# One down product behind the first plain tile, and the last norm's sums by VectorE and ScalarE

## Chip, core and metric

The kernel runs on one core of a Trainium2 chip. The metric is the device time of one execution in microseconds (us), as the median of several runs. TensorE (PE in the rows, PEld for its weight loads), VectorE (DVE), ScalarE (ACT), GpSimd (POOL) and the DMA queue of SyncE (SP) each work through their own instructions in order and wait for each other by semaphores.

## What is computed

One layer on 1024 tokens of width 1024, in float32 with products split into a high and a low part. What the change touches is the first and the third of its three residual steps and the norm behind the last:

```python
def layer_norm(x, g, b):
    mu = jnp.mean(xf, axis=-1, keepdims=True)
    var = jnp.mean(jnp.square(xf - mu), axis=-1, keepdims=True)
    y = (xf - mu) * lax.rsqrt(var + LN_EPS)
    return (y * g + b).astype(x.dtype)

def swiglu_ffn(x, w_gate, w_up, w_down):
    return (jax.nn.silu(x @ w_gate) * (x @ w_up)) @ w_down

x = layer_norm(ALPHA * x + 0.5 * swiglu_ffn(x, ...1), ln1_g, ln1_b)
x = layer_norm(ALPHA * x + hybrid_mixer(x, ...), ln2_g, ln2_b)
x = layer_norm(ALPHA * x + 0.5 * swiglu_ffn(x, ...2), ln3_g, ln3_b)
```

## The kernel before

Activations lie with features on the 128 partitions and tokens along the row, in halves of 512 tokens; each FFN (`Ffn`, once with `idx` 0 and once with `idx` 2) holds eight accumulators `acc[d][h]` per half. The order of TensorE's instructions is the order in which the code issues them (`run` walks a generator); the other engines' orders come from a scheduler that works with priorities, and `hoist()` raises one.

The down projection has two parts. `down` (L742) makes 2x2 block products with seven instead of eight multiplications over twelve of the 22 hidden tiles: for each item `(j0, m)` a PSUM tile `X` takes one product after the other, and after each of them `gather` (L693) adds `X` to an accumulator on VectorE (L696). The next product is added onto the same `X`, so TensorE may not start it before that addition has read `X`. In the loop another product always stands between two products onto the same tile. The last pass of the loop (`it` is None) has no item of its own any more: it issues the product with `s3` (9 matmuls, 3 tiles by 3 split terms), `gather`, then the product with `a22` (9 matmuls) and `gather`. With `idx` 2 a postponed product (`late_s1`) stands between these two; with `idx` 0 nothing does.

Behind `down`, `go` runs the plain tiles of the remaining hidden tiles (`plain`, L671): for each `d` 18 matmuls into a new PSUM tile of pool `dense` (4 slots), 6 hidden tiles by 3 split terms, with weights that `last_weights` splits on ScalarE and VectorE (L131, L132; the last two of a tile's six weight pieces lie in a shared tile `rest`), and hidden tiles that SP has fetched from DRAM (L794).

The last norm is done with tokens on the partitions. `TokenNorm.part(i)` transposes four accumulators to two PSUM tiles of 128 x 512, one for each 128 tokens (L363), and makes the sums `s` and the sums of squares `q`. In general `s` comes from a reduction on VectorE (L367) and `q` from a Square with an accumulated sum on ScalarE (L371). Only in the second part of the last 256 tokens (`own`) does TensorE make `s`: 8 products of an accumulator with a column of ones (L357), ahead of the transposes. `stats` (L386) then works on 128 x 2 numbers; `apply` (L399) makes four results from the four PSUM tiles (L402) and scales them (L411), and SP writes each to DRAM.

Of the kernel before, what the change touches and what calls it, by code (L numbers as in the profile page):

```python
# [8 lines left out]
F32 = mybir.dt.float32  # L9
# [3 lines left out]
AF = mybir.ActivationFunctionType  # L13
# [5 lines left out]
P = 128  # L19
# [48 lines left out]
def hybrid_layer(ctx, tc, xT, wg1, wu1, wds1, wd1, wg2, wu2, wds2, wd2, wcol, wnv, wgv, wdl, wgate,  # L68
                 wbr, wout, lnp, bias, dec2, bdec, ng, ident_d, masks_d, ln3, outN):
    nc = tc.nc  # L70
# [4 lines left out]
    def pool(stack, name, bufs=1, space=None):  # L75
        kw = dict(name=name, bufs=bufs)
        if space is not None:
            kw["space"] = space
        if space is not DRAM:
            kw["reuse_waits"] = "tile"  # L80
        return stack.enter_context(tc.tile_pool(**kw))
# [5 lines left out]
    lp = pool(ctx, "lp")  # L87
# [7 lines left out]
    def nm(s):  # L95
        uid[0] += 1
        return f"{s}_{uid[0]}"
# [29 lines left out]
    def dps(shape=(P, HF)):  # L127
        return dense.tile(list(shape), F32, tag="d", name=nm("d"))
# [46 lines left out]
    ones = cpool.tile([P, P], F32, tag="ones", name="ones")  # L175
# [13 lines left out]
    def run(*streams):  # L189
        for st_ in streams:  # L190
            for cost in st_:
                clock[0] += cost
                while pending and pending[0][0] <= clock[0]:
                    pending.pop(0)[2]()
# [134 lines left out]
    class TokenNorm:  # L329
# [20 lines left out]
        def part(self, i):  # L350
            s, q = ((self.s0, self.q0), (self.s1, self.q1))[i]
            own = i and self.t0 == S - TOK
            if own:
                self.s1 = s = dps((P, 2))
                for t in range(2):
                    for d in range(4):
                        nc.tensor.matmul(s[:, t:t + 1], self.z[4 + d][:, t * P:(t + 1) * P],  # L357
                                         ones[:, 0:1], start=d == 0, stop=d == 3)
            ps = [aux.tile([P, HF], F32, tag=t, name=nm("tz"), bufs=b)
                  for t, b in ((("pt", 1), ("o", 1)), (("s", 2), ("s", 2)))[i]]  # L360
            for d in range(4):
                for t in range(2):
                    nc.tensor.transpose(ps[t][:, d * P:(d + 1) * P],  # L363
                                        self.z[4 * i + d][:, t * P:(t + 1) * P], ident)
            for t in range(2):
                if not own:
                    nc.vector.tensor_reduce(s[:, t:t + 1], ps[t], axis=AX.X, op=ALU.add)  # L367
                if i == 0:
                    nc.vector.tensor_scalar(self.nc[:, t:t + 1], s[:, t:t + 1], -1.0 / HF, None,
                                            ALU.mult)  # L370
                nc.scalar.activation(self.tmp_(), ps[t], AF.Square, bias=self.nc[:, t:t + 1],  # L371
                                     accum_out=q[:, t:t + 1])
            if i == 0:
                self.ps = [ps]
                nc.vector.tensor_scalar(self.e, q, 0.25 / D, self.eps / 4, ALU.mult, ALU.add)
            else:
                self.ps.append(ps)
# [46 lines left out]
    def tagged(pl, tags, bufs):  # L424
        c = [0]

        def alloc(dt=F32):
            c[0] += 1
            t = tags[c[0] % len(tags)]
            return pl.tile([P, HF], dt, tag=t, name=nm(t), bufs=bufs)  # L430
        return alloc
# [7 lines left out]
    class Ffn:  # L439
# [287 lines left out]
        def down(self):  # L727
            prev, B, nxt = None, None, self.operands(0)
            self.wait = []
            items = [(j0, m) for j0 in range(0, PAIRS, NP) for m in range(4)]  # L730
            for it in [*items, None]:
                if it:
                    j0, m = it
                    if m == 0:
                        B, nxt = nxt, None
                    w = self.down_factors(j0, m)
                    if m == 1:
                        if j0 + NP < PAIRS:
                            nxt = self.operands(j0 + NP)
                        else:  # L740
                            for f in LAST:
                                self.fetch(f, 0)  # L742
                    X = dps()
                    yield from self.product(X, w["a11"], B[0], True)
                    self.gather(2 * m, 0, X)
                    Y = dps()
                    yield from self.product(Y, w["a12"], B[1], True)
                    self.gather(2 * m, 0, Y)
                if prev:
                    pm, pX, pw, pB = prev  # L750
                    yield from self.product(pX, pw["s3"], pB[5])
                    self.gather(2 * pm + 1, 1, pX)
                    if not it and self.idx:
                        yield from self.late_s1(self.wait[-1])
                late = it and j0 + NP == PAIRS and m > 1
                if late:
                    self.wait.append([m, w, B])
                elif it:
                    Z = dps()
                    yield from self.product(Z, w["s1"], B[3], True)  # L760
                    self.gather(2 * m + 1, 1, Z)
                if it:
                    yield from self.product(X, w["s2"], B[4])
                    self.gather(2 * m, 1, X)
                if prev:
                    yield from self.product(pX, pw["a22"], pB[6])
                    self.gather(2 * pm + 1, 0, pX)
                if it:
                    if not late:
                        yield from self.product(Z, w["s4"], B[2])  # L770
                        self.gather(2 * m, 1, Z)
                    prev = m, X, w, B
# [23 lines left out]
        def go(self, first, parts, sink_of):  # L796
            head = 2
            w2 = []
            for f in (0, 1):
                ws = first if f == 0 and first else self.gate_up(f)  # L800
                run(self.glu(f, ws, 0))
                w2.append(ws)
            for f in (0, 1):
                run(self.glu(f, w2[f], 1))
            for i in range(4):
                self.sums_of(i)
            run(self.blocks(range(head, FT)))
            self.front()
            run(self.down())
            idx, acc, tmp = self.idx, self.acc, self.tmp  # L810
            sums = tagged(self.hp, ("sr",), 4)
            dead = lambda dt=F32: xpool.tile([P, HF], dt, tag="x", name=nm("dead"))
            for f in LAST:
                self.fetch(f, 1)
            wr = self.last_weights()
            if idx:
                gb = [dead() for _ in range(4)]
                for i, t in enumerate(gb):
                    nc.sync.dma_start(t, ln3[0:1, i * HF:(i + 1) * HF].to_broadcast([P, HF]))
                token = lambda t0: TokenNorm(4 * LN_EPS, tmp, dead, gb, t0)  # L820
            for n, (h, c0, cn) in enumerate(parts):
                ln = None
                if idx == 0:
                    lags, gap = ln_lags[idx, h]
                    ln = Norm(cn, idx, 4 * LN_EPS, sums, tmp, sink_of(h, c0, cn), lags, gap)
                elif n == len(parts) - 1:
                    ln = token(h * HF + c0)
                for d in range(KD):
                    run(self.plain(LAST, d, next(wr) if n == 0 else self.wr[d], h, c0, cn))
                    if ln:  # L830
                        ln.add(acc[d][h][:, c0:c0 + cn])
                if not ln:
                    for i, c in enumerate(range(c0, c0 + cn, TOK)):
                        token(h * HF + c).later([acc[d][h][:, c:c + TOK] for d in range(KD)],
                                                TN_T0 + TN_DT * i)
                if n == 0:
                    run(self.deferred())
# [711 lines left out]
```

## Time and profile before

| | |
|---|---|
| Median of 3 runs | 2069.66 us (2068.62 to 2070.48) |
| The profiled execution | 2069.46 us, its span 2067.7 us |
| Granted TensorE clock, mean | 0.998 |
| PE busy, share of the span | 99% |
| PEld | 81% |
| DVE | 67% |
| ACT | 43% |
| POOL | 8% |
| DMA, mean | 155 GB/s |

The trace's times count from the span's start. In a timeline row the first two numbers are the start and the duration in us, then come engine, line, operation, tile written <- tiles read, the shape and, as xN, how many equal instructions the row merges; what stands in square brackets is the idle time of that engine just before, and what ended it.

### The profile page before, as it was taken

How to read it: one execution, taken by the hardware profiler on the slowest of the kernel's cores; microseconds unless marked ns; L12 is line 12 of the kernel's file. 1: busy time of each engine (PE TensorE's matmuls, PEld its weight loads, DVE VectorE, ACT ScalarE, POOL GpSimd, SP SyncE). 2: the span in 40 equal slices, each digit the busy share in tenths (PEclk: the TensorE clock that was granted, in tenths of full speed). 3: DMA queues.
4: the chain of work that ended last, by engine and by line, in shares of the span. 5: the costliest groups of instructions: out<-in, count | busy, mean ns of one | idle time of the engine just before them, and what ended most of it. 6: DMA issues, size and time to landing. Idle time of an engine off the chain costs nothing.

```text
span 2067.7 us, 26798 instructions
## 1 busy us (share of the span) xinstructions
PE 2046.2 (99%) x9738; PEld 1684.6 (81%) x9738; DVE 1378.0 (67%) x2355; ACT 896.1 (43%) x1502; POOL 159.1 (8%) x243
## 2 busy tenths in 40 slices
PE   9999999999999999999999999999999999999998
PEld 7888888888888788877788888887888888888888
DVE  8676776547668875236557755799767777457647
ACT  6444444322224554346656544355544444322212
POOL 0000000000013221213100000132000000000000
PEclk9999999999999999999999999999999999999999
DMA  4343444386641354488543336421334443396622
GB/s 145 141 164 131 170 149 134 128 286 248 227 137 49 109 194 138 138 235 228 156 119 107 110 126 194 133 83 73 135 138 153 166 157 126 122 326 220 239 100 83
DMA packets 159765, 321.37 MB, mean 155 GB/s; under 512 B 18448, under 2 KB 42768, under 8 KB 159632
## 3 DMA queue, kind: packets, MB, share of 16 engines
q1 hardware_dynamic: 140304, 274.03, 39.3%
q0 software_dynamic: 9216, 29.37, 4.9%
q10 hardware_dynamic: 10112, 16.26, 2.5%
q8 instruction: 77, 1.26, 0.3%
q14 instruction: 56, 0.46, 0.1%
HBM read 222.19 MB, written 101.06 MB: 156 GB/s over the span
## 4 chain that ended last, share of the span: by engine, by line
PE 83%; issue 6%; DVE 5%; POOL 2%; DMA 2%; ACT 1%; SPq 0%; ACTq 0%; POOLq 0%; DVEq 0%
PE d L569 16%; PE d L567 16%; PE d L568 16%; PE d L122 6%; PE d L124 6%; PE d L123 6%; PE d L674 3%; PE d L676 3%; PE d L675 3%; PE pt L1126 1%; PE po L1143 1%; POOL xl L420 1%; POOL qks L912 1%; DMA gv<-sl 1%; PE d L898 1%
## 5 line engine op out<-in xcount | busy, mean ns | idle before, releaser
L131 ACT ACTIVATE wh<-raw 128x512 fp32r<-128x512 f32 (+4 forms) x148 | 111.5, 763 | 187.6 <-PE d L568 85.4
L132 DVE TENSOR_TENSOR wl<-raw,wh 128x512 fp32r<-128x512 f32 (+4 forms) x148 | 125.3, 854 | 100.4 <-ACT wh L131 100.2
L696 DVE TENSOR_TENSOR a<-a,d 128x512 f32<-128x512 f32 (+1 forms) x152 | 99.9, 657 | 93.8 <-PE d L569 64.7
L123 PE MATMUL d<-xl,wh 128*128 128x512 f32 x384 | 150.7, 392 | 3.6 <-POOL xl L420 3.1
L122 PE MATMUL d<-xh,wh 128*128 128x512 f32 x384 | 153.6, 400 | 0.2
L124 PE MATMUL d<-xh,wl 128*128 128x512 f32 x384 | 150.4, 392 | 0.5 <-DVE wl L112 0.5
L569 PE MATMUL d<-hh,hl 128*128 128x512 f32 x384 | 149.5, 389 | 0.0
L569 PE MATMUL d<-xh,wl 128*128 128x512 f32 x384 | 149.5, 389 | 0.0
L568 PE MATMUL d<-xl,wh 128*128 128x512 f32 x384 | 149.4, 389 | 0.0
L567 PE MATMUL d<-hh,hh 128*128 128x512 f32 x384 | 149.4, 389 | 0.0
L567 PE MATMUL d<-xh,wh 128*128 128x512 f32 x384 | 149.4, 389 | 0.0
L567 PE MATMUL d<-a,wh 128*128 128x512 f32 x384 | 149.4, 389 | 0.0
L568 PE MATMUL d<-a,wh 128*128 128x512 f32 x384 | 149.4, 389 | 0.0
L569 PE MATMUL d<-a,wl 128*128 128x512 f32 x384 | 149.4, 389 | 0.0
L568 PE MATMUL d<-hl,hh 128*128 128x512 f32 x384 | 149.4, 389 | 0.0
L131 ACT ACTIVATE hh<-sr 128x512 fp32r<-128x512 f32 x168 | 105.9, 631 | 83.6 <-DVE sr L508 24.2
L674 PE MATMUL d<-hh,wh 128*128 128x512 f32 (+1 forms) x368 | 134.3, 365 | 0.0
L676 PE MATMUL d<-hh,wl 128*128 128x512 f32 (+1 forms) x368 | 133.0, 361 | 0.0
L675 PE MATMUL d<-hl,wh 128*128 128x512 f32 (+1 forms) x368 | 133.0, 361 | 0.0
L132 DVE TENSOR_TENSOR hl<-sr,hh 128x512 fp32r<-128x512 f32 x168 | 114.9, 698 | 2.2 <-ACT hh L131 1.4
L112 DVE TENSOR_TENSOR wl<-raw,wh 128x512 fp32r<-128x512 f32 (+1 forms) x77 | 81.1, 1054 | 46.6 <-ACT wh L111 42.7
L131 ACT ACTIVATE oh<-hr 128x512 fp32r<-128x512 f32 x88 | 55.4, 631 | 128.4 <-DVE hr L599 44.3
(339 smaller groups left out, 4900.9 us busy)
## 6 DMA issues: line engine op xcount, KB each, us to landing
raw<-in_wu SPq DMA_DIRECT2D x44, 512.0 KB
raw<-in_wg SPq DMA_DIRECT2D x43, 512.0 KB
ops<-oh SPq DMA_DIRECT2D x84, 256.0 KB
ops<-ol SPq DMA_DIRECT2D x84, 256.0 KB
oh<-ops SPq DMA_DIRECT2D x48, 256.0 KB
ol<-ops SPq DMA_DIRECT2D x48, 256.0 KB
hid<-oh SPq DMA_DIRECT2D x40, 256.0 KB
hid<-ol SPq DMA_DIRECT2D x40, 256.0 KB
```

The source lines that it names most:

```text
L122: nc.tensor.matmul(ps, a, xh, start=k == 0, stop=False)
L123: nc.tensor.matmul(ps, a, xl, start=False, stop=False)
L124: nc.tensor.matmul(ps, wl[:, k * m:(k + 1) * m], xh, start=False, stop=k == n - 1)
L131: nc.scalar.activation(hi, src, AF.Copy)
L132: nc.vector.tensor_tensor(lo, src, hi.bitcast(F32), ALU.subtract)
L567: nc.tensor.matmul(ps, a, xh, start=first and k == 0, stop=False, **sg)
L568: nc.tensor.matmul(ps, a, xl, start=False, stop=False, **sg)
L569: nc.tensor.matmul(ps, wl[:, k * P:(k + 1) * P], xh, start=False, stop=k == n - 1, **sg)
L674: nc.tensor.matmul(ps, wh, hi, start=k == 0, stop=False)
L675: nc.tensor.matmul(ps, wh, lo, start=False, stop=False)
L676: nc.tensor.matmul(ps, wl, hi, start=False, stop=k == n - 1)
L696: nc.vector.tensor_tensor(a, a, ps, ALU.add)
```

## The change

Two edits.

First: in the last pass of `down` the `a22` product and its `gather` are no longer issued there when `idx` is 0 but kept as a generator, `self.rest`, and `go` runs it behind the first plain tile of the first block.

Second: for `own`, the 8 products with ones are dropped. `s` becomes an SBUF tile `ln_s1` of pool `lp`; its column 0 comes from a VectorE reduction of the first transposed tile, its column 1 from a ScalarE Copy with an accumulated sum over the second, issued ahead of the two Squares. In the built program `lp` grows by 32 bytes in each partition for it, and the pools opened later (`hp` of both FFNs, and those of the mixer) start 32 bytes further on.

```diff
@@ TokenNorm.part
             if own:
-                self.s1 = s = dps((P, 2))
-                for t in range(2):
-                    for d in range(4):
-                        nc.tensor.matmul(s[:, t:t + 1], self.z[4 + d][:, t * P:(t + 1) * P],
-                                         ones[:, 0:1], start=d == 0, stop=d == 3)
+                self.s1 = s = lp.tile([P, 2], F32, tag="ln_s1", name=nm("ln_s1"), bufs=1)
...
+            if own:
+                nc.scalar.activation(self.tmp_(), ps[1], AF.Copy, accum_out=s[:, 1:2])
             for t in range(2):
-                if not own:
+                if not own or t == 0:
                     nc.vector.tensor_reduce(s[:, t:t + 1], ps[t], axis=AX.X, op=ALU.add)
@@ Ffn.down
                 if prev:
-                    yield from self.product(pX, pw["a22"], pB[6])
-                    self.gather(2 * pm + 1, 0, pX)
+                    def last(pm=pm, pX=pX, pw=pw, pB=pB):
+                        yield from self.product(pX, pw["a22"], pB[6])
+                        self.gather(2 * pm + 1, 0, pX)
+                    if it or self.idx:
+                        yield from last()
+                    else:
+                        self.rest = last()
@@ Ffn.go
                     run(self.plain(LAST, d, next(wr) if n == 0 else self.wr[d], h, c0, cn))
+                    if not (n or d or idx):
+                        run(self.rest)
```

Line numbers of the changed kernel are lower by 2 in most of the code (L696 is L694 there), by 4 for the transposes (L359). In what follows `d_4937` is the tile `X` of the last item, `oh` the hidden operands, `a_4000` and `a_3968` the accumulators of its two last additions. On TensorE, before, around the end of `down` of the first FFN:

```order
L569 MATMUL d_4937<-oh_4276,wl_4911 128x512
L567 MATMUL d_4937<-oh_4280,wh_4910 128x512
L568 MATMUL d_4937<-ol_4281,wh_4910 128x512
...
L569 MATMUL d_4937<-oh_4288,wl_4911 128x512
L674 MATMUL d_5043<-hh_4720,wh_5036 128x512
```

And after the change, where `d_5033` is the first plain tile:

```order
L567 MATMUL d_4937<-oh_4276,wl_4911 128x512
L672 MATMUL d_5033<-hh_4720,wh_5026 128x512
...
L674 MATMUL d_5033<-hh_4740,wl_5024 128x512
L565 MATMUL d_4937<-oh_4280,wh_4910 128x512
L566 MATMUL d_4937<-ol_4281,wh_4910 128x512
```

The 18 matmuls of the plain tile now stand between the last matmul with `s3` and the first with `a22`. On VectorE, at the same place, before:

```order
L696 TENSOR_TENSOR a_4000<-a_4000,d_4937 128x512
L132 TENSOR_TENSOR wl_5096<-raw_5094,wh_5095 128x512
L696 TENSOR_TENSOR a_3968<-a_3968,d_4937 128x512
L132 TENSOR_TENSOR wl_5034<-raw_5094,wh_5033 128x256
L132 TENSOR_TENSOR wl_5125<-raw_5123,wh_5124 128x512
L132 TENSOR_TENSOR wl_5034<-raw_5123,wh_5033 128x256
L696 TENSOR_TENSOR a_3724<-a_3724,d_5043 128x512
```

And after:

```order
L694 TENSOR_TENSOR a_4000<-a_4000,d_4937 128x512
L132 TENSOR_TENSOR wl_5096<-raw_5094,wh_5095 128x512
L132 TENSOR_TENSOR wl_5024<-raw_5094,wh_5023 128x256
L132 TENSOR_TENSOR wl_5125<-raw_5123,wh_5124 128x512
L694 TENSOR_TENSOR a_3724<-a_3724,d_5033 128x512
L132 TENSOR_TENSOR wl_5024<-raw_5123,wh_5023 128x256
L694 TENSOR_TENSOR a_3968<-a_3968,d_4937 128x512
```

The addition of the plain tile (`a_3724`) moved ahead of one weight split, the addition of the `a22` product behind it. At the end of the program, on VectorE before (`tz` are the transposed tiles, `d_17924` the product with ones):

```order
L387 TENSOR_TENSOR ln_sm_17685<-ln_sm_17685,d_17924 128x2
L402 SCALAR_TENSOR_TENSOR dead_17681<-tz_17865,ln_sm_17685,dead_17121 128x512
...
L402 SCALAR_TENSOR_TENSOR dead_17684<-tz_17934,ln_sm_17685,dead_17122 128x512
L394 RECIPROCAL ln_sm_17685<-ln_sm_17685 128x2
L395 TENSOR_TENSOR ln_sm_17685<-ln_sm_17685 128x2
```

And after:

```order
L365 TENSOR_REDUCE ln_s_3851_17924<-tz_17925 128x1
L385 TENSOR_TENSOR ln_sm_17685<-ln_sm_17685,ln_s_3851_17924 128x2
L400 SCALAR_TENSOR_TENSOR dead_17681<-tz_17865,ln_sm_17685,dead_17121 128x512
...
L392 RECIPROCAL ln_sm_17685<-ln_sm_17685 128x2
L400 SCALAR_TENSOR_TENSOR dead_17684<-tz_17926,ln_sm_17685,dead_17122 128x512
L393 TENSOR_TENSOR ln_sm_17685<-ln_sm_17685 128x2
```

A reduction is new ahead of the first small operation, and the fourth result operation now stands behind the first reciprocal instead of ahead of it.

## Rows read from the trace of the kernel before

**Rows 1.** Page, part 1: busy us (share of the span) xinstructions.

```profile
PE 2046.2 (99%) x9738; PEld 1684.6 (81%) x9738; DVE 1378.0 (67%) x2355; ACT 896.1 (43%) x1502; POOL 159.1 (8%) x243
```

**Rows 2.** PE's waits, whole span: engine line <- releaser: us, times, longest.

```profile
PE d L898 <- POOL xl L420: 2.2, 3, 0.7
...
PE d L567 <- DVE a L696: 0.9, 1, 0.9
```

**Rows 3.** Timeline, PE and DVE at the end of the first `down`.

```profile
577.68 0.39 PE L567 MATMUL d<-oh,wh 128*128 128x512 f32 x1
...
582.21 0.39 PE L569 MATMUL d<-oh,wl 128*128 128x512 f32 x1
...
582.64 0.69 DVE L696 TENSOR_TENSOR a<-a,d 128x512 f32<-128x512 f32 x1 [0.68 <-PE d L569]
...
583.47 0.47 PE L567 MATMUL d<-oh,wh 128*128 128x512 f32 x1 [0.87 <-DVE a L696]
...
585.63 0.39 PE L674 MATMUL d<-hh,wh 128*128 128x512 f32 x1
```

**Rows 4.** Timeline: what the first plain tile reads, and the load after it.

```profile
569.48 0.69 DVE L132 TENSOR_TENSOR wl<-raw,wh 128x512 fp32r<-128x512 f32 x1 [0.44 <-ACT wh L131]
...
577.07 0.32 SPq L794 DMA_DIRECT2D hl<-hid  x1
...
581.20 0.76 DVE L132 TENSOR_TENSOR wl<-raw,wh 128x256 fp32r<-128x256 f32 x2
...
584.77 1.88 ACT L131 ACTIVATE wh<-raw 128x512 fp32r<-128x512 f32 x4 [3.67 <-DMA raw<-in_wd]
```

**Rows 5.** Timeline: VectorE's weight splits behind the gap.

```profile
586.64 1.36 DVE L132 TENSOR_TENSOR wl<-raw,wh 128x256 fp32r<-128x256 f32 x3
```

**Rows 6.** Timeline, the tail: last plain matmul, last addition, ones, transposes.

```profile
2055.26 0.28 PE L676 MATMUL d<-hh,wl 128*128 128x256 f32 x1
...
2055.58 0.42 DVE L696 TENSOR_TENSOR a<-a,d 128x256 f32<-128x256 f32 x1 [1.31 <-PE d L676]
...
2056.06 0.63 PEld L357 LDWEIGHTS d<-ones,a 128*128 128x128 f32 x5
...
2057.20 1.07 PE L363 MATMUL tz<-ident,a 128*128 128x128 f32 x8
```

**Rows 7.** Timeline, the tail: VectorE and ScalarE up to the last scaling.

```profile
2057.37 0.16 DVE L387 TENSOR_TENSOR ln_sm<-ln_sm,d 128x2 f32<-128x2 f32 x1 [1.37 <-PE d L357]
...
2058.19 0.69 ACT L371 ACTIVATE hr<-tz,ln_sm 128x512 f32<-128x512 f32 x1 [4.12 <-PE tz L363]
...
2058.50 1.41 DVE L402 SCALAR_TENSOR_TENSOR dead<-tz,ln_sm,dead 128x512 f32<-128x512 f32 x2
2058.78 0.19 ACT L371 ACTIVATION_READ_ACCUMULATOR hr<-tz,ln_sm 128x1 f32 x1
...
2060.55 0.16 DVE L394 RECIPROCAL ln_sm<-ln_sm 128x2 f32<-128x2 f32 x1
2060.74 0.16 DVE L395 TENSOR_TENSOR ln_sm<-ln_sm 128x2 f32<-128x2 f32 x1
...
2061.33 2.74 DVE L411 SCALAR_TENSOR_TENSOR dead<-dead,ln_sm,dead 128x512 f32<-128x512 f32 x4
```

**Rows 8.** Timeline: reductions and accumulated sums in earlier parts of this norm.

```profile
2029.13 1.29 DVE L367 TENSOR_REDUCE ln_sm<-tz 128x1 f32<-128x512 f32 x2 [0.34 <-PE tz L363]
...
2029.92 0.69 ACT L371 ACTIVATE hr<-tz,ln_sm 128x512 f32<-128x512 f32 x1 [0.21 <-DVE ln_sm L367]
...
2053.87 0.20 ACT L371 ACTIVATION_READ_ACCUMULATOR hr<-tz,ln_sm 128x1 f32 x1
...
2054.10 0.17 DVE L375 TENSOR_SCALAR ln_sm<-ln_sm 128x2 f32<-128x2 f32 x1 [0.26 <-ACT hr L371]
```

**Rows 9.** Page, part 5: matmuls on tiles of `hp`: line, shapes xcount | busy, mean ns.

```profile
L569 PE MATMUL d<-hh,hl 128*128 128x512 f32 x384 | 149.5, 389 | 0.0
...
L674 PE MATMUL d<-hh,wh 128*128 128x512 f32 (+1 forms) x368 | 134.3, 365 | 0.0
```

## The prediction

> **What bounds the kernel now.** Page part 1 first: TensorE is busy 99% of the span, the next engine 67% [rows 1]. So time is won only where TensorE stands still, or behind its last instruction. The view of TensorE's waits comes next, because it lists every stop by what ended it: all are small, and exactly one is of the kind that the first edit touches, a matmul of L567 that waited once, 0.9 us, for the addition L696 [rows 2]. The timeline around it shows the size: matmuls follow each other at 0.2265 us (20 steps from 577.68 to 582.21), the last one with `s3` starts at 582.21, so the first with `a22` was due at 582.44; it starts at 583.47, 0.14 behind the end of the addition that reads the same PSUM tile [rows 3]. For the second edit the last stretch is read, engine by engine: from 2055.26, where the last plain matmul starts, to 2061.33, where VectorE begins the last scalings [rows 6, 7]. After that come four scalings and four writes that neither edit touches; they move with their start.
>
> **The first edit.** It adds and removes no instruction, it moves nine matmuls and one addition. What goes: 583.47 - 582.44 = 1.03 us of standing still. The restart was slow as well: from the first matmul with `a22` to the first plain one it took 2.16 us [rows 3] where nine steps are 2.04, so 0.12 more. Together **1.15 us**; 1.03 is the lower bound if a similar slow pair turns up at the new places.
>
> Whether a new wait takes its place: the plain tile now starts at 582.44 instead of 585.63, 3.2 us earlier. It reads, in order, four weight pieces whose low parts VectorE began to make at 569.48, then two pieces from the tile `rest`, whose low parts were done at 581.96 and which are due 12 steps in, at 585.16 [rows 4]. Its hidden tiles were fetched by SP ahead of a run of loads of which the last was issued at 577.07, and ScalarE took up weights from a load that SP issued behind all of these at 584.77 [rows 4]; the last hidden tile is due 15 steps in, at 585.84. So the operands are there with a microsecond or more to spare, by the latest bound as well. Its PSUM slot has been read by an addition that stands ahead of the one at 582.64 on VectorE. The `a22` product then starts 18 steps after the `s3` product ends, 4 us behind an addition that takes 0.7. Behind it the second plain tile needs nothing new.
>
> On VectorE the addition of the plain tile waits for TensorE until about 586.7 and holds one weight split behind it. Before, the three splits there ran from 586.64 to 588.00 [rows 5]; now one of them follows the addition, at about 587.5, and the slot of raw weights that it frees comes free at about 588 as before. No SP load is held back by that. The accumulator of the `a22` product is next touched by a plain tile some 24 us later. Cost of the moves: nothing, hidden under plain tiles whose weights are ready several us ahead.
>
> **The second edit.** TensorE loses 16 passes (each of the 8 products in two), from 2055.26 to the transposes: these began at 2057.20 and can now begin at 2055.38. That is 1.8 us less on TensorE, but not on the end. The last accumulator is ready only when L696 ends, at 2056.00; the weight load that needed it ran at 2056.06 [rows 6]. Transposes start every 0.113 us (seven steps in 1.07 less the 0.28 of the last), so six of them, from 2055.38, just fit ahead of that. So the seventh starts at 2056.06, the eighth at 2056.17. Before, the seventh started at 2057.88 and ScalarE 0.31 later at 2058.19 [rows 6, 7]; I take 0.31 for both readers.
>
> VectorE: reduction from 2056.37, 0.69 long [rows 8], usable at 2057.06. ScalarE: Copy from 2056.48; the nearest row is the Square of the same shape, whose accumulator is read 0.59 after its start [rows 7], and VectorE uses such a sum 0.23 after the read starts [rows 8]. So `L387` can run at 2056.48 + 0.59 + 0.23 = **2057.30**. Before, it ran at 2057.37. The 1.8 us have become 0.07.
>
> From there VectorE is full: L387 to L411 took 3.96 us [rows 7], in which it makes four results of 0.66 to 0.7 each and ten small operations. The same work follows now. One change of order helps: the fourth result operation comes between the first reciprocal and the operation that waits 0.19 for it [rows 7], which covers about 0.1 of that. L411 then starts at 2057.30 + 3.86 = 2061.16, a gain of 0.17, say **0.2 us**. ScalarE isn't late for this: the first Square waits for the reduction of its tile, 0.79 after that starts as in an earlier part [rows 8], at 2057.16, which is also when the Copy lets go; the second Square's sum is there at about 2058.7, and VectorE asks for it at about 2059.1. Bounds: 0.43 gained if only the reduction counts (2057.06); 0.25 lost if the handover from ScalarE takes 0.3 to 0.4 more than in [rows 8]. Two engines reading two PSUM tiles at once is not new: the Square at 2058.19 ran beside a result operation and took its usual 0.69 [rows 7].
>
> The Trainium skill ("Perfetto Trace Analysis", section "Optimizing Scalar/DVE Operations") gives VectorE about 125 ns of access overhead on PSUM and ScalarE about 51. By that the ScalarE half would be the shorter one, by an estimated 74 ns, the reduction would decide, and the second edit would be worth 0.43 instead of 0.2. The trace disagrees: with its separate accumulator read the ScalarE sum is usable 0.82 after its start, the reduction after 0.69.
>
> **Sum.** Against the profiled execution: 2069.46 - 1.15 - 0.17 = 2068.14. That execution lies 0.20 under the median of the runs, so the forecast for a median is **2068.3 us**.
>
> **Rivals.**
> - The stop in front of TensorE only moves. Later it waits three times, 2.2 us in all, for GpSimd's low parts behind the first norm [rows 2]. If that chain is paced by something that the edit doesn't move, TensorE arrives 1.15 earlier and waits 1.15 longer. For it: GpSimd and VectorE are busy there. Against it: the norm's steps are started by plain tiles, all of which move. Time: 2069.66 - 0.2 = 2069.5. The other way not to do what it says, a plain tile that waits for its operands, gives the same time at most, and rows 4 speak against it.
> - The tail gains what TensorE gives up less the accumulator's wait: if VectorE were not full between L387 and L411, the end would follow the Squares, which finish 1.03 earlier (2058.19 + 0.68 for the second, against 2057.84 now). Against it: the rows of VectorE there lie end to end. Time: 2069.66 - 1.15 - 1.03 = 2067.5.
> - The tail loses: the side-by-side sums come late by the upper bound. Time: 2069.66 - 1.15 + 0.25 = 2068.8.
> - Slower: the 32 bytes. All tiles of `hp` now start at another place in each partition, and these are moving operands of at least 2256 matmuls (three rows of 384 and three of 368, of which [rows 9] shows one each). If reading them cost TensorE more, the gain would be gone at 1.32 / 2256 = 0.6 ns for each, and at 2.4 ns the kernel would be slower by over 0.2%; at 1% of the 226.5 ns step it would be 2069.66 - 1.32 + 5.1 = 2073.4, at 2% 2078.5. For it: no row shows this start. Against it: 512 columns take 389 ns from tiles of this pool and of the others alike, and a matmul's pace is set by its columns.
>
> **How the numbers follow.** Forecast 0.65; gain absorbed 0.15; tail gains more 0.08; tail loses 0.07; the 32 bytes 0.05, split into 0.03 for slower by over 0.2% and 0.02 for a gain of that size, as I have no sign for it. A measurement of this kernel can tell about 0.2%, 4.1 us, from no change, and the whole of both edits is 1.3 us: so same 0.95, slower 0.03, faster 0.02. The range reaches from 2067.5 less half a microsecond of spread between medians (the runs shown spread over 1.9 us) to 2069.5 plus that: 2067.0 to 2070.0.
>
> **What would show it.** Right: no wait of L567 for L696 in the view of TensorE's waits; the first plain tile starts 0.23 after the last `s3` matmul; L387's releaser is ScalarE's accumulated sum, 2.0 us behind the start of the last plain matmul (2.1 before); L387 to L411 takes 3.8 to 3.9 us. Wrong: a plain matmul that waits for `hh`, `hl` or `wl`; a longer wait of L898; L387 released later than 2.2 us behind the last plain matmul; a mean above 389 ns for the matmuls on `hh` and `hl`.

## The result: 14.8 us slower, and the profile after

The changed kernel takes **2084.64 us** in the median (2084.05 to 2085.27, 6 runs); the kernel before took 2069.82 us beside it (2068.62 to 2070.74, 6 runs). The ratio is 1.0072, 95% interval 1.0062 to 1.0082: slower by 14.8 us. The forecast was 2068.3 us with a range up to 2070.0, so it was wrong. The rival "the 32 bytes", which had a chance of 0.05 (0.03 of it for slower), is what happened, and the experiments below show that it accounts for the loss.

Line numbers of the changed kernel are two lower from L365 to L694, the transposes four lower (L567 to L569 are now L565 to L567, L674 to L676 are L672 to L674, L363 is L359), and five higher from L901 on. The first line of part 1 of its profile page, from an execution with a span of 2083.5 us and a granted clock of 0.998, answers to [rows 1]:

```profile
PE 2062.1 (99%) x9722; PEld 1682.1 (81%) x9722; DVE 1381.5 (66%) x2356; ACT 897.1 (43%) x1504; POOL 158.2 (8%) x243
```

TensorE has 16 instructions fewer than before and is busy 15.9 us longer. So the lost time is not a wait; TensorE's work itself takes longer. Its waits (line waiting <- what ended the wait: us in total, times, longest) confirm it:

```profile
PE d L123 <- POOL xl L418: 2.4, 4, 0.7
PE d L903 <- POOL xl L418: 2.1, 3, 0.7
PE pz L156 <- DVE wz L153: 1.2, 1, 1.2
PE pl L269 <- DVE sl L253: 1.1, 1, 1.1
```

The wait for the addition in `down` [rows 2], 0.9 us, is no longer in this view, and no new one of its size has come. What got longer is seen where matmuls are grouped by line, tiles and shape (count | busy us, mean ns of one). First six of these rows from the trace of the kernel before:

```profile
L567 PE MATMUL d<-xh,wh 128*128 128x512 f32 x384 | 149.4, 389 | 0.0
L568 PE MATMUL d<-hl,hh 128*128 128x512 f32 x384 | 149.4, 389 | 0.0
L674 PE MATMUL d<-hh,wh 128*128 128x512 f32 x272 | 106.7, 392 | 0.0
L567 PE MATMUL d<-xh,hh 128*128 128x512 f32 x192 | 74.7, 389 | 0.0
L674 PE MATMUL d<-hh,wh 128*128 128x256 f32 x96 | 27.6, 287 | 0.0
L676 PE MATMUL d<-hh,wl 128*128 128x256 f32 x96 | 27.1, 283 | 0.0
```

And after the change:

```profile
L565 PE MATMUL d<-xh,wh 128*128 128x512 f32 x384 | 149.5, 389 | 0.0
L566 PE MATMUL d<-hl,hh 128*128 128x512 f32 x384 | 149.3, 389 | 0.0
L672 PE MATMUL d<-hh,wh 128*128 128x512 f32 x272 | 108.4, 398 | 0.0
L674 PE MATMUL d<-hh,wl 128*128 128x512 f32 x272 | 107.4, 395 | 0.0
L565 PE MATMUL d<-xh,hh 128*128 128x512 f32 x192 | 75.8, 395 | 0.0
L672 PE MATMUL d<-hh,wh 128*128 128x256 f32 x96 | 27.3, 284 | 0.0
L674 PE MATMUL d<-hh,wl 128*128 128x256 f32 x96 | 26.8, 279 | 0.0
```

In `d<-X,Y` the first tile, X, is the moving one and Y holds the weights. `xh` over `wh` (no tile has moved) and `hl` over `hh` (both have moved by 32 bytes) take 389 ns as before. `hh` over `wh` and `xh` over `hh`, where one of the two has moved and the other hasn't, take 6 ns more than the 392 and 389 of before. This suggests that it isn't the place of `hp`'s tiles that costs time but the **distance between the start of the moving tile and the start of the weights' tile**. The rows of 256 columns went the other way, from 287 and 283 ns to 284 and 279; they are few.

The timeline shows the same at one place of the first `down` stage, with the weight loads. The load for the next matmul starts with the matmul now running and takes 0.19 us of it:

```profile
588.35 0.39 PE L567 MATMUL d<-oh,wl 128*128 128x512 f32 x1
588.35 0.19 PEld L672 LDWEIGHTS d<-hh,wh 128*128 128x128 f32 x1
588.57 0.40 PE L672 MATMUL d<-hh,wh 128*128 128x512 f32 x1
588.77 0.69 DVE L694 TENSOR_TENSOR a<-a,d 128x512 f32<-128x512 f32 x1 [0.68 <-PE d L567]
588.81 0.39 PE L673 MATMUL d<-hl,wh 128*128 128x512 f32 x1
...
592.54 0.40 PE L674 MATMUL d<-hh,wl 128*128 128x512 f32 x1
592.77 0.39 PE L565 MATMUL d<-oh,wh 128*128 128x512 f32 x1
```

The first plain matmul starts 0.22 behind the last one with `s3`, without a gap: the first edit does what it was meant to do. From there 18 steps of the plain tile take 4.20 us, 233.3 ns each; before, this tile took 4.09 us from 585.63 [rows 3] on, 227.2 ns each.

The tail is the last place to compare (TensorE, VectorE and ScalarE from the last plain matmul to the last scalings):

```profile
2071.41 0.28 PE L674 MATMUL d<-hh,wl 128*128 128x256 f32 x1
2071.53 1.11 PE L359 MATMUL tz<-ident,a 128*128 128x128 f32 x8
2072.57 0.69 DVE L365 TENSOR_REDUCE ln_s<-tz 128x1 f32<-128x512 f32 x1 [0.42 <-PE tz L359]
2072.68 0.60 ACT L362 ACTIVATE hr<-tz 128x512 f32<-128x512 f32 x1 [2.36 <-PE tz L359]
2073.17 0.19 ACT L362 ACTIVATION_READ_ACCUMULATOR hr<-tz 128x1 f32 x1
...
2073.40 0.16 DVE L385 TENSOR_TENSOR ln_sm<-ln_sm,ln_s 128x2 f32<-128x2 f32 x1
...
2077.22 2.74 DVE L409 SCALAR_TENSOR_TENSOR dead<-dead,ln_sm,dead 128x512 f32<-128x512 f32 x4
```

L385 runs 1.99 behind the last plain matmul (2.11 before, [rows 6, 7]) and the last scalings 5.81 behind it (6.07 before): 0.26 us gained, not lost.

### The profile page after: what moved, and what is told of

It is laid out like the page before. It is cut to its first block, busy times and chain, and to the rows that moved or that the text cites. A ratio compares the mean times of both kernels' runs of the same rounds, so it can differ in the third digit from the quotient of the medians.

```text
span 2083.5 us, 26769 instructions
## 1 busy us (share of the span) xinstructions
PE 2062.1 (99%) x9722; PEld 1682.1 (81%) x9722; DVE 1381.5 (66%) x2356; ACT 897.1 (43%) x1504; POOL 158.2 (8%) x243
## 4 chain that ended last, share of the span: by engine, by line
PE 93%; DVE 3%; DMA 1%; issue 1%; ACT 1%; POOL 1%; SPq 0%; DVEq 0%; POOLq 0%; ACTq 0%
PE d L567 18%; PE d L565 18%; PE d L566 18%; PE d L122 6%; PE d L124 6%; PE d L123 6%; PE d L672 4%; PE d L674 4%; PE d L673 4%; PE d L903 1%; PE pt L1131 1%; PE d L901 1%; PE d L902 1%; PE po L1148 1%; DVE wl L112 1%
## 5 line engine op out<-in xcount | busy, mean ns | idle before, releaser
L694 DVE TENSOR_TENSOR a<-a,d 128x512 f32<-128x512 f32 (+1 forms) x152 | 99.9, 657 | 95.6 <-PE d L567 67.8
L123 PE MATMUL d<-xl,wh 128*128 128x512 f32 x384 | 150.7, 393 | 3.1 <-POOL xl L418 2.4
L567 PE MATMUL d<-hh,hl 128*128 128x512 f32 x384 | 150.3, 391 | 0.0
L567 PE MATMUL d<-a,wl 128*128 128x512 f32 x384 | 150.1, 391 | 0.0
L565 PE MATMUL d<-hh,hh 128*128 128x512 f32 x384 | 150.1, 391 | 0.0
L565 PE MATMUL d<-a,wh 128*128 128x512 f32 x384 | 149.8, 390 | 0.0
L565 PE MATMUL d<-xh,wh 128*128 128x512 f32 x384 | 149.5, 389 | 0.0
L567 PE MATMUL d<-xh,wl 128*128 128x512 f32 x384 | 149.5, 389 | 0.0
L672 PE MATMUL d<-hh,wh 128*128 128x512 f32 (+1 forms) x368 | 135.6, 369 | 0.0
L674 PE MATMUL d<-hh,wl 128*128 128x512 f32 (+1 forms) x368 | 134.2, 365 | 0.0
```

The costliest lines, as they stand in the source:

```text
L123: nc.tensor.matmul(ps, a, xl, start=False, stop=False)
L565: nc.tensor.matmul(ps, a, xh, start=first and k == 0, stop=False, **sg)
L567: nc.tensor.matmul(ps, wl[:, k * P:(k + 1) * P], xh, start=False, stop=k == n - 1, **sg)
L672: nc.tensor.matmul(ps, wh, hi, start=k == 0, stop=False)
L674: nc.tensor.matmul(ps, wl, hi, start=False, stop=k == n - 1)
```

## The experiments

**The theory.** While a matmul of 512 columns streams its moving tile, the weights of the next one are loaded, as the timeline above shows. The step from one matmul to the next depends on how far the starts of these two tiles lie apart in a partition, modulo 256 bytes. In the built program of the kernel before, all large tiles start at 64 modulo 256; in that of the changed kernel the tiles of `hp` and of the pools behind it start at 96. Weights are read in pieces of 128 columns, 512 bytes, of a tile, so that the piece doesn't enter. **Rivals:** the tiles' absolute start; the banks of PSUM, which the removed sums shift for some `d` tiles; the edits themselves.

Two of the experiments are the changed kernel with a wider `ln_s1` (below with 64 bytes), and eight are the kernel before with a spare tile that is allocated in a chosen pool, cleared once by GpSimd and never read. N is its size in numbers of 4 bytes (the pool rounds it up to a multiple of 32 bytes):

```diff
-                self.s1 = s = lp.tile([P, 2], F32, tag="ln_s1", ...)
+                self.s1 = s = lp.tile([P, 16], F32, tag="ln_s1", ...)[:, :2]
```

```diff
     nc.scalar.activation(ones_r, ones, AF.Copy)
+    pad = lp.tile([P, N], F32, tag="pad", name="pad")
+    nc.gpsimd.memset(pad, 0.0)
```

For each, the mean start-to-start step was worked out from the timeline of TensorE, over all stretches of at least six successive steps on the same two pools. That gives the table to which the paragraphs below refer. "hh over w": the moving tile lies in `hp` or in the mixer's pool behind it, and a tile `wh` or `wl` is loaded meanwhile (1484 steps; 281 of them load from the tiles `wh` and `wl` that `last_weights` puts into the x pool); "x over hh" (573); "x over w" (some 4060, `a` and `oh` tiles included); "hh over hh" (1224). The last column is the median less that of the kernel before, run beside it.

| kernel | `hp` later by | hh over w | x over hh | x over w | hh over hh | us |
|---|---|---|---|---|---|---|
| before | 0 | 226.8 ns | 226.7 | 227.2 | 226.8 | |
| changed | 32 B | 233.3 | 233.1 | 227.8 | 228.0 | +14.8 |
| before + 32 | 32 | 233.3 | 233.1 | 227.8 | 228.0 | +17.3 |
| changed, 64 wide | 64 | 229.1 | 232.9 | 227.9 | 228.8 | +9.9 |
| before + 96 | 96 | 233.4 | 233.6 | 228.1 | 229.0 | +20.5 |
| before + 128 | 128 | 232.9 | 232.9 | 227.9 | 226.9 | +15.3 |
| before + 160 | 160 | 234.1 | 233.9 | 228.2 | 228.7 | +20.7 |
| before + 192 | 192 | 233.3 | 229.1 | 227.8 | 227.2 | +13.3 |
| before + 224 | 224 | 233.3 | 233.4 | 227.6 | 228.0 | +16.2 |
| changed, 256 wide | 256 | 226.8 | 226.7 | 227.3 | 226.8 | -1.6 |
| all pools + 32 | 32, and all others | 226.8 | 226.7 | 227.2 | 226.7 | +0.1 |
| weights and `hp` + 32 | 32, and the weights | 228.1 | 233.4 | 233.3 | 227.9 | +31.5 |

### The kernel before with 32 bytes more, and no edit

The spare tile in `lp`, N = 2.

> The kernel before with one more 8-byte tile (32 once rounded) in `lp`, cleared once by GpSimd; neither edit is in it, PSUM is as before. Relative-start theory: `hp` and the pools behind it shift by 32 bytes as in the changed kernel, so the matmuls on pairs of a shifted and an unshifted tile take 395 instead of 389 ns: 2085.9 us (2084.5 to 2087), which is the changed kernel's time plus the 1.3 us that the two edits were to save. Rival of the PSUM banks, and rival that the edits themselves cost the time: no change, 2069.8.

Measured: 2086.84 us, ratio 1.0083 (1.0068 to 1.0098). Its groups by shape are those of the changed kernel:

```profile
L570 PE MATMUL d<-hl,hh 128*128 128x512 f32 x384 | 149.3, 389 | 0.0
L676 PE MATMUL d<-hh,wh 128*128 128x512 f32 x272 | 108.3, 398 | 0.0
L569 PE MATMUL d<-xh,hh 128*128 128x512 f32 x192 | 75.8, 395 | 0.0
```

A tile that nobody reads makes the kernel 17.3 us slower, with PSUM as before and neither edit in it. The steps of the table account for it: 1484 x 6.5 + 573 x 6.4 + 4062 x 0.6 + 1224 x 1.2 ns = 17.2 us, and the small groups nearly cancel. The PSUM banks and the edits are out as causes.

### The first edit alone

The kernel before with the first part of the change's diff, the `last` generator that `go` runs behind the first plain tile.

> The first edit alone: last product with `a22` behind the first plain tile, norm sums as before, so no tile of SBUF moves and PSUM is as before. Relative-start theory: no slow matmuls, and the first edit brings the 1.15 us of the prediction: 2068.7 us (2068 to 2069.5). Rival (the moved product upsets the stages behind it): near 2084.

Measured: 2068.31 us, 1.23 less than before; ratio 0.9994 (0.9985 to 1.0004). No tile moves in it, and nothing is slow.

### All pools 32 bytes later

The spare tile stands in `cpool`, N = 2, ahead of all the pools with large tiles.

> The kernel before with the extra 32 bytes in `cpool`, ahead of the pools of `x`, `a`, `w`, `lp` and `hp`: all of them shift by 32 bytes together, so that pairs of tiles keep their distance and each of them alone starts elsewhere; no edit. Relative-start theory: about 2070 us (2069 to 2071.5), since only products with the constants change their distance. Rival, absolute start (every operand that starts off a multiple of 64 bytes costs 7 ns): some 9000 matmuls slow, about +60 us, 2130.

Measured: 2069.66 us, ratio 1.0000 (0.9991 to 1.0010):

```profile
L570 PE MATMUL d<-hl,hh 128*128 128x512 f32 x384 | 149.4, 389 | 0.0
L676 PE MATMUL d<-hh,wh 128*128 128x512 f32 x272 | 106.7, 392 | 0.0
L569 PE MATMUL d<-xh,hh 128*128 128x512 f32 x192 | 74.7, 389 | 0.0
```

Every row is back at its value of before, though `hp` starts where it does in the changed kernel. The absolute start doesn't matter, at least for a move of 32 bytes, and the clearing by GpSimd, which is in this kernel too, costs nothing.

### The weights and `hp` 32 bytes later, x and a not

The spare tile stands in a pool of its own ahead of the weight pool.

> The kernel before with the extra 32 bytes ahead of the weight pool: tiles of `wpool`, `lp` and `hp` shift by 32 bytes together, those of the x and a pools stay; no edit. Relative-start theory: products of `hh` with `wh` are at the old pace (389 ns), products of `xh` or `a` with `wh` are slow (395 ns), some 4100 pairs, and some 780 of x tiles with `hh` or of `wh` with x tiles as well: 4900 x 7 ns = 34 us, less for the weights that lie in the x pool, so 2095 to 2106. Rival (it is the tiles of `hp` alone that must start at the old place): L674 to L676 slow as in the changed kernel, the x products fast, 2086.

Measured: 2101.17 us, ratio 1.0153 (1.0139 to 1.0167). Now the other pairs are slow:

```profile
L570 PE MATMUL d<-xh,wh 128*128 128x512 f32 x384 | 151.9, 396 | 0.0
L571 PE MATMUL d<-hl,hh 128*128 128x512 f32 x384 | 150.0, 391 | 0.0
L677 PE MATMUL d<-hh,wh 128*128 128x512 f32 x272 | 107.3, 394 | 0.0
```

`xh` over `wh`, 389 ns before and in the changed kernel, has become slow without `xh` having moved; `hh` over `wh`, slow in the changed kernel, is within 2 ns of before. Expected was a full return, 389 and 392 where 391 and 394 were measured.

The remainder on `hh` over `wh` has a place. In the plain tiles behind `down`, four of the six weight pieces lie in tiles that `last_weights` takes from the x pool (`xtile("wh")`), which didn't move here; the last two lie in `rest`, in the weight pool, which moved with `hp`. In the timeline L679 at 2030.73 is the last matmul on a piece in the x pool, L679 at 2032.09 the last on one in `rest`, and L679 at 2034.89 the last on the next tile's pieces in the x pool:

```profile
2030.73 0.39 PE L679 MATMUL d<-hh,wl 128*128 128x512 f32 x1
...
2032.09 0.40 PE L679 MATMUL d<-hh,wl 128*128 128x512 f32 x1
...
2034.89 0.39 PE L679 MATMUL d<-hh,wl 128*128 128x512 f32 x1
```

The six steps in which a piece of `rest` is loaded take 1.36 us, 226.7 ns each; the twelve in which one of the x pool is loaded take 2.80, 233.3 each. Over the whole span the steps of `hp` tiles take 226.8 ns where a piece of the weight pool is loaded (872 steps), as before, and 233.3 where one of the x pool is (281): in one and the same loop, the place of the weights decides. The 228.1 of the table is a mean over both.

### Other distances

First the changed kernel with `ln_s1` 64 bytes wide, run beside the first three kernels above:

> The changed kernel with its small sums tile made 64 bytes wide instead of 8 (32 once rounded), so that the tiles of `hp` and of the pools behind it start 64 bytes later than in the kernel before, not 32. Relative-start theory (a matmul is about 7 ns slower where its moving tile and the weight tile loaded beside it start 32 bytes apart in the partition): the pairs are 64 apart again, the loss is gone, both edits remain: 2068.4 us (2067.5 to 2069.5), L674 to L676 (L672 to L674 in the changed kernel) at 389 ns. If the pattern repeats only after 128 or 256 bytes: still about 2084. Rival of the PSUM banks (the removed sums in PSUM moved `d` to other banks): the banks are as in the changed kernel, so 2084.6.

Measured: 2079.46 us, ratio 1.0048 (1.0033 to 1.0063). Neither number: the pattern isn't one of 64 bytes. Its steps show why it lies between: with `hh` over the weights only a third of the loss is left (229.1), with x tiles over `hh` all of it (232.9). The distance has opposite signs in these two. So four more distances were tried, with N = 32, 56, 24 and 40 in `lp`, and, to test the sign, N = 48.

> The kernel before with a spare tile of 128 bytes in `lp`; `hp` shifts by 128 bytes, no edit. At a distance of 32 bytes the loss was 17.3 us, at 64 about 11. If the pattern repeats every 128 bytes: 2069.5, no loss. If it repeats only every 256 bytes or more, or falls with the distance: a loss between 1 and 11 us, 2071 to 2081.

Measured: 2084.98 us, ratio 1.0074 (1.0059 to 1.0090), above the expected range; at 128 bytes both signs are the same distance, and both kinds of pairs take 232.9 ns.

> The kernel before with a spare tile of 224 bytes in `lp`; `hp` shifts by 224 bytes, which is 32 bytes short of the old start modulo 256; no edit. If the distance counts in both directions alike: the same loss as with 32 bytes, 2086.8 (2085 to 2088). If only a start that is a little later than the other tile's costs time: no loss, 2069.5. The pairs in which x tiles move over `hh` weights have the opposite sign to those in which `hh` moves over `wh`, so a one-sided rule would leave one of the two kinds slow: 2073 to 2083.

Measured: 2085.90 us, ratio 1.0079 (1.0065 to 1.0092): as with 32 bytes, both kinds slow.

> The kernel before with a spare tile of 192 bytes in `lp`; no edit. Over whole stretches of matmuls of 512 columns the step was 226.8 ns at distance 0; with the moving tile 64 bytes ahead of the weights' start (modulo 256, `hh` over `wh`) 229.1, with it 64 bytes behind (`xh` over `hh`) 232.9. Here the two change places. Theory that direction and size of the distance, and nothing else of the tiles, set the step: `hh` over `wh` 232.9, `xh` over `hh` 229.1, so 2069.7 + 1484 x 6.1 ns + 573 x 2.4 ns + about 3 for the other pairs = 2083 (2081.5 to 2085). Rival (the pair of pools matters, not the direction): steps and time as at 64 bytes, 2080.7.

Measured: 2082.98 us, ratio 1.0066 (1.0044 to 1.0089). The two kinds have changed places, 233.3 and 229.1 ns: sign and size of the distance set the step, not the pools.

> The kernel before with a spare tile of 96 bytes in `lp`; no edit. If the step is lowest where the starts agree modulo 256 and high everywhere else: 229 to 233.5 ns for `hh` over `wh`, 2079 to 2087. Rival (some other distance is better than 0): steps under 226 ns, under 2069.

> The kernel before with a spare tile of 160 bytes in `lp`; no edit. This is the distance of 96 bytes in the other direction. If starts that agree modulo 256 are best: 229 to 233.5 ns for the pairs of `hp` and other tiles, 2079 to 2087. Rival (some other distance is better than 0): under 2069.

Measured: 2090.20 us (1.0098, 1.0069 to 1.0127) and 2090.36 us (1.0099, 1.0069 to 1.0128). Of the distances tried for `hp` alone these two cost most, and no distance in steps of 32 bytes is better than 0.

### The changed kernel with the distance restored

`ln_s1` is 256 bytes wide (`[P, 64]`), so `hp` starts at 64 modulo 256 again; both edits are in it.

> The changed kernel with its small sums tile 256 bytes wide, so that the tiles of `hp` start 256 bytes later than in the kernel before and their start modulo 256 is the old one. Relative-start theory with a period of at most 256 bytes: every matmul at the old pace, and both edits show as predicted: 2068.3 us (2067.3 to 2069.3), the side-by-side sums worth 0.2 of it beside the first edit's 1.2. Rival (the 10 us that stayed at a distance of 64 bytes came from the edits, not from the distance): about 2079.

Measured: **2068.13 us** (2067.48 to 2068.81, 11 runs) against 2069.69; ratio 0.9992 (0.9983 to 1.0001). Part 1 of its page, its group on `hh`, and the first place:

```profile
PE 2044.0 (99%) x9722; PEld 1682.5 (81%) x9722; DVE 1378.6 (67%) x2356; ACT 896.8 (43%) x1504; POOL 158.8 (8%) x243
```

```profile
L672 PE MATMUL d<-hh,wh 128*128 128x512 f32 x272 | 106.7, 392 | 0.0
```

```profile
582.47 0.39 PE L567 MATMUL d<-oh,wl 128*128 128x512 f32 x1
582.47 0.19 PEld L672 LDWEIGHTS d<-hh,wh 128*128 128x128 f32 x1
582.70 0.39 PE L672 MATMUL d<-hh,wh 128*128 128x512 f32 x1
```

TensorE is busy 18.1 us less than in the changed kernel, with the same 9722 instructions; 224 bytes that nobody reads are the whole difference. Of all the kernels here this one has the lowest time: 1.56 us under the kernel before beside it, the first edit alone 1.23 under its own. Neither can be told from the kernel before with certainty, since both intervals reach just past 1. The 17.3 us of the spare tile less this 1.56 come to 15.7, and the changed kernel lost 14.8; the difference is within the intervals.

## Why the prediction was wrong

- **What bounds the kernel** was read rightly: TensorE's own work. That is why 3% on some 2200 matmuls arrived in the time almost undiminished.
- **The first edit** was right in mechanism and size. The wait for L694 is gone, the first plain matmul starts 0.22 to 0.23 behind the last one with `s3`, and no plain matmul waits. Forecast 1.15 us, measured alone 1.23, though with an interval that doesn't exclude nothing.
- **The gain absorbed later:** no. L903 waits 2.1 us for GpSimd (2.2 before, at L898), and in the kernel with the distance restored L123 waits 3.1 us for GpSimd, as it did before (`PE d L123 <- POOL xl L420: 3.1, 4, 1.2` in the view of the waits).
- **The second edit** was a little undersized. L385 runs 1.99 behind the last plain matmul (forecast 2.04), L385 to L409 takes 3.82 (forecast 3.86); together 0.26 gained, forecast 0.17. The sum on ScalarE is there 0.72 after the Copy starts, forecast 0.82, because the Copy takes 0.60 and not the 0.69 of the Square, which I had taken as the nearest row. The Trainium skill ("Perfetto Trace Analysis", section "Optimizing Scalar/DVE Operations") puts ScalarE's access to PSUM below VectorE's by an estimated 74 ns; the Copy and VectorE's reduction do differ in that direction, 0.60 against 0.69, but a Square of the same shape on ScalarE takes 0.69 as well, so these rows don't show that the access makes the difference. ScalarE's sum is still the later one: its own read of the accumulator, 0.19 long, stands behind it. The upper bound of 0.43 for the tail comes to 0.41 from its own rows (0.24 between 2057.06 and 2057.30, and the 0.17).
- **The sum without the 32 bytes** was thus right: 2068.3 forecast, 2068.13 measured once the distance is restored, though that interval, too, doesn't exclude that nothing was gained.
- **The step that failed** is the rival of the 32 bytes, and in it the sentence against it: "512 columns take 389 ns from tiles of this pool and of the others alike, and a matmul's pace is set by its columns". Every row of 389 ns [rows 9] came from tiles that start at 64 modulo 256. So these rows showed one distance, 0, and could say nothing of another; I took agreement at one point for independence. Nor is it the reading of these tiles that got dearer, as the rival had it: with all pools moved together they are at 389 ns again, and the distance to the weights decides. The rival was priced within sight of the truth (2078.5 us at 2% for 2256 matmuls; measured 6.5 ns, 2.9%), but that the number of matmuls fitted is luck. Of my 2256, 1152 have `hh` or `hl` as weights too, at distance 0 (389 to 391 ns), and 288 have 256 columns; in their place came pairs that I hadn't counted: x tiles over `hh`, `hh` over `wh` in `down`, and the mixer's tiles, some 2200 slow steps in all. A chance of 0.05 for a state that no row shows, on the engine that is busy for 99% of the span, was the error, and so was a range that left its price out.

The prediction named the sign by which it would fall, a mean above 389 ns on `hh` and `hl`, and that is what the trace showed, though not for `hl` over `hh`.

## What to carry to other kernels

Whoever adds even a small tile ahead of large ones should look where the large ones start afterwards: on a kernel bound by TensorE, keep the moving tiles of matmuls like these (512 columns) and their weight tiles at the same start modulo 256 bytes, by widening the new tile or by placing it behind them. When a change moves something that every instruction of the bounding engine touches, ask whether any row of the trace shows it in another place; if none does, its price belongs in the range.

## What was not expected of the hardware

- A matmul of 512 columns takes a step of 226.8 ns where its moving tile and the weights loaded meanwhile start at the same place modulo 256 bytes. With the moving tile 64 bytes further on it takes 229.1, at the other multiples of 32 bytes 232.9 to 234.1. Distances that aren't multiples of 32 bytes weren't tried.
- With 256 columns it is the other way: 119.8 ns at distance 0, 117.1 at 32 bytes, 117.8 at 64, and 117.6 to 119.9 at the other distances, of which the one of 96 gains nothing. These are 277 steps here.
- The tile which counts is, by nearly all steps at a distance of 32 bytes, the one being loaded for the next matmul, not the one in use. In the kernel with the weights and `hp` moved, the step from the last piece in the x pool onto the first in `rest`, where only the weights in use are off, takes 227.7 ns (23 steps); the step back, where only the weights loaded are off, 235.0 (21 steps). In the changed kernel, `a` over `wl` with `hh` loading and `hh` over `hl` with `wh` loading take 235.0 (45 steps each, 226.6 before). One kind of step doesn't fit: `xh` over `hl` with `wh` loading takes 232.7 against 226.6 (45 steps), where only the weights in use are off. It is the first step behind a change of pair, where steps can vary, as the next point shows; that this is the reason here isn't shown.
- Pairs at distance 0 also take 0.1 to 2.2 ns more in the mean in nearly every kernel in which other pairs are off (the columns "x over w" and "hh over hh"). For "hh over hh" this lies in the first steps behind a pair that is off. In the 48 long stretches of it in the changed kernel the first seven steps take 224.4 to 235.8 ns, and from the eighth on they are at 226.7, as before; in the other kernels that have such pairs it takes one to ten steps, and behind them all are at 226.7.
- Left open: why a stretch needs some steps to settle there, while the plain tiles in the kernel with the weights moved are at 226 to 227 ns within one or two. Nor does any run here show what in the chip makes two starts collide; the runs show only that their distance decides.
